# Relative bias table, overflow loop, last down weights and last norm of a decoder layer on one core

## Chip, core and metric

The kernel runs on one core of a Trainium2 chip. The metric is device time in microseconds (us). TensorE (PE) does the matmuls, PEld are its weight loads, VectorE is DVE, ScalarE is ACT, GpSimd is POOL; SyncE (SP) issues nearly all DMAs. Every engine works through its own instructions in order.

## What is computed

One layer of a decoder on 256 tokens of width 1024, in float32: attention with eight heads and a causal relative bias, a norm, then a mixture of 32 experts of which each token takes four, and a last norm. The reference, cut:

```python
s_own = einsum('bhqd,bhjd->bhqj', qc, ko) * scale + rel_t[:, t5_bucket(rel_own)]
s_own = where(rel_own >= 0, s_own, -inf)          # causal
x = layer_norm(alpha * x + softmax(s_own) @ v @ w_out)
top_logit, top_e = top_k(x @ w_router + b_router, 4); gate = softmax(top_logit)
# per expert: h = x @ w_gu[e] + b_gu[e]; act = swiglu(h); y = act @ w_down[e] + b_down[e]
out = layer_norm(alpha * x + sum(gate * y))
```

## The kernel before

The order of all work is written out by hand. Weights come in chunks of 2 MB, one for each slot: a pool has 13 slots of 128 x 4096 floats, of which two hold long-lived tiles (`BT_xT`, `QT_KTt`) through the expert part, so that up to 11 hold weights. `todo` is the list of chunks in order: six blocks of the input projection (`in`), two of the output projection, then for each expert four chunks `gu` (gate and up) and two `dn` (down). `prefetch` issues the next chunk on SP whenever a slot is free beyond `reserve[0]`; `done` frees a slot and calls it. Each DMA is given one of eight semaphores in turn (`DMAHW0` to `DMAHW7` in the order below) and is issued when the previous one on that semaphore has landed, so that at most eight are under way.

Attention: `split` turns each weight block into a high and a low part (a cast on ACT, a subtraction on DVE); steps n = 0 to 11 of a loop (`proj_qk`, `proj_v`) multiply half a block each. The bias reaches the softmax through DRAM: `rel_bias` multiplies the one-hot buckets by the table on PE, `rel_bias_out` writes the result as 8 rows of 383 numbers to `rd`, and `rel_bias_in` reads it back as the tile `BT`, 128 partitions of 8 heads x 256, each partition one place further on. Write and read are issued by ACT in steps n = 2 and 3. `softmax` of the first head needs `BT` in step 5.

Experts: each has 64 places. `stage1` multiplies by gate and up, `swiglu` makes the activation, `act_T` transposes it into `aT`, `stage2` multiplies by down into `Y`. Experts go in pairs; `pair_scatter` adds a pair's result to `acc` by a matmul with the gates `GT`, during the next pair. Choices beyond 64 places would be done by `more_blocks`, a loop whose number of turns is read from `n_i` at run time by every engine; with these inputs it has no turn. It stands behind expert 31, and is followed by the last pair's scatter and the last norm (`mean_neg`, `variance`, `centre`, `inverse_root`, `finish`), mostly on DVE. `spread_gain` makes the norm's gain and bias of all partitions during expert 30. The last chunk (`dn` of expert 31) is fetched in four pieces.

Of the kernel before, what the change touches and what calls it, by code (L numbers as in the profile page):

```python
# [11 lines left out]
F32 = mybir.dt.float32  # L12
# [11 lines left out]
NE, TOPK = 32, 4  # L24
# [36 lines left out]
def tile_decoder_layer(ctx: ExitStack, tc, a, out):  # L61
# [78 lines left out]
    def prefetch():  # L140
        while todo and W_SLOTS - used[0] > reserve[0]:
            fetch(1 if len(todo) > 1 else 4)
# [83 lines left out]
    BT, QT, KTt = (t.rearrange("p (h s) -> p h s", h=H) for t in (BT, QT, KTt))  # L226
# [3 lines left out]
    rrow = hp.tile([H, 383], F32, name="rrow")  # L230
# [6 lines left out]

    xT3 = xT.rearrange("p (k s) -> p k s", k=KT)
# [18 lines left out]
    nc.vector.memset(rrow[:, 0:127], NEG)  # L257
    nc.vector.memset(zeros, 0.0)
    rd = dr.tile([H, 383], F32, name="rd")

    def rel_bias():
        pr = bank("tp2")
        nc.tensor.matmul(pr[:H, :256], rb, oh, start=True, stop=True)
        nc.vector.tensor_copy(rrow[:, 127:383], pr[:H, :256])
        nc.sync.dma_start(c, a["consts"])
        nc.sync.dma_start(router.rearrange("p k e -> p (k e)"), a["router"])
# [87 lines left out]
    def softmax(hh):  # L354
# [39 lines left out]
    for n in range(12):  # L394
# [4 lines left out]
        if n == 1:  # L399
            rel_bias()  # L400
            reserve[0] = 1
            prefetch()
        if n == 2:
            rel_bias_out()
        if n == 3:
            rel_bias_in()
# [248 lines left out]
    def pair_gather(OH):  # L655
        xg = biases[:, :1024].rearrange("p (k c) -> p k c", k=KT)
# [34 lines left out]
    def act_T(act):  # L691
# [5 lines left out]
    def stage2(aT, chunk, swap, Y, after, apart=False):  # L697
        banks = [bank(n) for n in (("yp", "hg") if apart else ("yp",))]
        y_ps = [banks[s * apart][s * 64:(s + 1) * 64] for s in range(2)]
# [8 lines left out]
        for s, copy in enumerate((nc.scalar.copy, nc.vector.tensor_copy if apart else nc.scalar.copy)):  # L708
            copy(Y[s * 64:(s + 1) * 64, s ^ swap, :], y_ps[s])  # L709
# [77 lines left out]
    def more_blocks():  # L787
# [4 lines left out]
        GT2 = spare[:, 1024:1536].rearrange("p (b t c) -> p b t c", b=2, t=2)  # L792
        itn = small("itn", 1)
# [3 lines left out]
        with tc.For_i(0, n_reg, 1):  # L797
# [23 lines left out]
            OH = mp.tile([128, 2, 2, CAP], F32, name="OH")  # L821
            Gd = mp.tile([128, 2, 2, 2, CAP], F32, name="Gd")
# [6 lines left out]
            xg, quarter = pair_gather(OH)  # L829
# [21 lines left out]
            for t in range(2):  # L851
                for cb in range(2):
# [9 lines left out]
    for p in range(NE // 2):  # L862
        ahead_pair = p + 1 < NE // 2
        for s in range(2):
# [14 lines left out]
            reserve[0] = int(e == 14)  # L879
# [7 lines left out]
            if e == 21:  # L887
                overflow_list()
            if look_ahead:
# [12 lines left out]
            if e == NE - 2:  # L902
                gb2, sq = halves(slot("gb2_sq"))
                spread_gain()
            stage2(aT, lambda j: take(("dn", e, j)), s, Y, lambda j: done(("dn", e, j)), apart=e == NE - 1)
    more_blocks()
    nc.scalar.preload_act_table(AF.Sqrt)


    sm = [mp.tile([128, 8], F32, name=f"sm{t}") for t in range(2)]  # L910
    sq = sq[:, :D]

    def mean_neg(t):
        for cb in range(2):
            po = o_tile()
            nc.tensor.matmul(po, GT[:, cb, t, :], Y[:, cb, :], start=True, stop=True)  # L916
            d = acc[:, t, HALVES[cb]]
            nc.vector.scalar_tensor_tensor(d, po, 1.0, d, op0=OP.mult, op1=OP.add,  # L918
                                           accum_out=sm[t][:, cb:cb + 1])
        nc.vector.tensor_scalar(sm[t][:, 2:3], sm[t][:, 0:1], sm[t][:, 1:2], -1.0 / D, op0=OP.add, op1=OP.mult)  # L920

    def variance(t):
        nc.scalar.activation(sq, acc[:, t], AF.Square, bias=sm[t][:, 2:3], accum_out=sm[t][:, 3:4])
        nc.scalar.activation(sm[t][:, 4:5], sm[t][:, 3:4], AF.Sqrt, scale=1.0 / D, bias=eps)

    def centre(t, s, on_vector=False):
        d, m, g = acc[:, t, s], sm[t][:, 2:3], gb2[:, :D][:, s]
        if on_vector:
            nc.vector.scalar_tensor_tensor(d, d, m, g, op0=OP.add, op1=OP.mult)  # L929
        else:  # L930
            nc.scalar.activation(d, d, AF.Identity, bias=m)
# [71 lines left out]
```

## Time and profile before

| | us |
|---|---|
| median of 3 runs | 1087.15 (1087.0 to 1087.31) |
| profiled execution, its own time | 1087.11 |
| its span, first to last instruction | 1085.3 |
| PE busy | 975.1 (90%) |
| DVE busy | 265.6 (24%) |
| ACT busy | 180.5 (17%) |
| moved by DMA | 425.74 MB, mean 392 GB/s |

Rows are read so: an entry such as `PE o L310` is an engine, the tile it writes and the source line; what stands in brackets at the end of a row is the engine's idle time before it and what ended it. Starts count from the first instruction of the span. Lines are those of the kernel before.

### The profile page before, as it was taken

The page shows a single profiled execution, that of the slowest core. Times are in us where ns is not written, and L with a number is a line of the kernel's source. Part 1 is how long each engine was busy: PE and PEld are TensorE (multiplying, and loading weights), DVE is VectorE, ACT ScalarE, POOL GpSimd, SP SyncE. Part 2 cuts the span into 40 slices and gives each one's busy share as a digit, 9 for nine tenths or more (in the row PEclk, how much of TensorE's full clock was granted, in tenths as well). Part 3 has the DMA queues.
Part 4 walks back from the last instruction along what each step waited for, and adds up shares of the span by engine and source line. Part 5 has one row for each costly group of instructions (what it writes and reads, how often), then busy time and mean ns, then how long its engine had stood idle before and what let it go on. Part 6 is the DMA issues. An engine that isn't in the chain of part 4 may idle for free. (4 is left out here: it accounts for less than half of the span.)

```text
span 1085.3 us, 11473 instructions
## 1 busy us (share of the span) xinstructions
PE 975.1 (90%) x4886; PEld 450.4 (41%) x4886; DVE 265.6 (24%) x555; ACT 180.5 (17%) x345; POOL 15.7 (1%) x10
## 2 busy tenths in 40 slices
PE   9649989999999999888989889999989898988893
PEld 8648764334343443232424243343423243333331
DVE  5237562121222211112121232212111212121104
ACT  5126431101011110010101010011101010101112
POOL 0000030000000000000000000000000000000001
PEclk9869989999999999999999989999999999999997
DMA  9964579999999999999999999999999999999981
GB/s 358 422 243 152 161 297 406 428 427 428 428 426 428 428 425 430 427 427 429 426 429 428 413 423 426 428 428 427 427 428 427 428 429 428 428 428 426 429 372 40
DMA packets 33204, 425.74 MB, mean 392 GB/s; under 512 B 3672, under 2 KB 5120, under 8 KB 7456
## 3 DMA queue, kind: packets, MB, share of 16 engines
q1 hardware_dynamic: 31824, 422.87, 92.8%
q10 hardware_dynamic: 1328, 2.11, 0.6%
q8 instruction: 40, 0.66, 0.2%
q14 instruction: 12, 0.10, 0.0%
HBM read 423.91 MB, written 1.06 MB: 392 GB/s over the span
## 5 line engine op out<-in xcount | busy, mean ns | idle before, releaser
L677 PE MATMUL hg<-w,QT_KTt 128*64 128x512 f32 x960 | 250.8, 599 | 54.5 <-DMA w<-in_w_gu 54.2
L677 PE MATMUL hu<-w,QT_KTt 128*64 128x512 f32 x960 | 248.6, 594 | 0.0
L705 PE MATMUL yp<-w,QT_KTt 128*64 128x512 f32 x1008 | 226.8, 595 | 1.3 <-ACT QT_KTt L695 1.3
L684 DVE TENSOR_SCALAR QT_KTt<-hg 128x512 f32<-128x512 f32 x32 | 22.1, 692 | 665.5 <-PE hg L677 665.5
L677 PEld LDWEIGHTS hg<-w,QT_KTt 128*64 128x64 f32 x960 | 66.0, 137 | 194.9 <-issue 127.0
L705 PEld LDWEIGHTS yp<-w,QT_KTt 128*64 128x64 f32 x1008 | 70.6, 137 | 142.3 <-issue 127.9
L677 PEld LDWEIGHTS hu<-w,QT_KTt 128*64 128x64 f32 x960 | 71.2, 137 | 135.7 <-issue 135.7
L685 ACT ACTIVATE QT_KTt<-QT_KTt 128x512 f32<-128x512 f32 x32 | 20.1, 629 | 477.7 <-DVE QT_KTt L684 477.7
L709 ACT COPY QT_KTt<-yp 64x512 f32<-64x512 f32 x63 | 36.5, 580 | 233.4 <-PE yp L705 225.9
L663 PEld LDWEIGHTS tp<-OH,BT_xT 128*128 128x128 f32 x480 | 58.4, 199 | 12.0 <-issue 11.2
L663 PE MATMUL tp<-OH,BT_xT 128*128 128x128 f32 x480 | 62.7, 286 | 0.0
L165 DVE TENSOR_TENSOR whl<-w,whl 128x1024 fp32r<-128x1024 f32 (+1 forms) x36 | 41.2, 1187 | 29.4 <-ACT whl L176 29.4
L310 PE MATMUL o<-xhl,whl 128*128 128x256 f32 x48 | 15.0, 312 | 25.1 <-DVE QT_KTt L320 24.5
L176 ACT CAST whl<-w 128x1024 fp32r<-128x1024 f32 (+1 forms) x36 | 32.7, 954 | 11.3 <-DMA w<-in_w_in 4.7
L569 DVE TENSOR_SCALAR QT_KTt<-tp,c 128x128 f32<-128x128 f32 x60 | 20.5, 405 | 44.1 <-PE tp L663 44.1
L733 PE MATMUL tp<-QT_KTt 128*128 128x512 f32 x60 | 30.7, 593 | 0.0
L733 PE MATMUL o<-QT_KTt 128*128 128x512 f32 x60 | 29.8, 618 | 0.0
L571 ACT ACTIVATE QT_KTt<-tp,c 128x128 f32<-128x128 f32 x60 | 22.6, 457 | 36.3 <-PE tp L663 36.3
L695 ACT COPY QT_KTt<-tp 128x512 f32<-128x512 f32 x32 | 19.2, 600 | 42.9 <-PE tp L694 35.9
L686 DVE TENSOR_SCALAR hu<-hu 128x512 f32<-128x512 f32 x32 | 22.4, 700 | 3.1 <-PE hu L677 0.2
L694 PE MATMUL tp<-c,QT_KTt 128*128 128x128 f32 x128 | 20.0, 280 | 3.4 <-DVE QT_KTt L688 3.2
L688 DVE SCALAR_TENSOR_TENSOR QT_KTt<-hu,QT_KTt 128x512 f32<-128x512 f32 x32 | 22.1, 691 | 1.1
(258 smaller groups left out, 758.7 us busy)
## 6 DMA issues: line engine op xcount, KB each, us to landing
w<-in_w_gu SPq DMA_DIRECT2D x128, 2048.0 KB, 39.1
w<-in_w_dn SPq DMA_DIRECT2D x63, 2048.0 KB, 39.1
w<-in_w_in SPq DMA_DIRECT2D x3, 2048.0 KB, 21.1
w<-in_w_in SPq DMA_DIRECT2D x4, 1024.0 KB, 11.1
w<-in_w_out SPq DMA_DIRECT2D x2, 2048.0 KB, 28.3
w<-in_w_dn SPq DMA_DIRECT2D x4, 512.0 KB, 31.8
w<-in_w_in SPq DMA_DIRECT2D x4, 256.0 KB, 5.7
w<-in_w_in SPq DMA_DIRECT2D x2, 512.0 KB, 8.5
```

The lines of the kernel that those rows point to most:

```text
L165: nc.vector.tensor_tensor(lo[:, s], w[:, s], hi[:, s].bitcast(F32), op=OP.subtract)
L176: nc.scalar.copy(o, i)
L569: nc.vector.tensor_scalar(o, i, g, b, op0=OP.mult, op1=OP.add)
L571: nc.scalar.activation(o, i, AF.Identity, scale=g, bias=b)
L663: nc.tensor.matmul(ps[:, k * 128:(k + 1) * 128], h[:, t, kk * 128:(kk + 1) * 128], OH[:, t].rearrange("p s c -> p (s c)"), start=t == 0, s ...
L677: nc.tensor.matmul(hgu[i][s * 64:(s + 1) * 64], xg(k), w[:, kk, q * 512:(q + 1) * 512], start=False, stop=k == KT - 1)
L684: nc.vector.tensor_scalar(g7, hgu[0], LIMIT, None, op0=OP.min)
L686: nc.vector.tensor_scalar(u7, u7, LIMIT, -LIMIT, op0=OP.min, op1=OP.max)
L688: nc.vector.scalar_tensor_tensor(sg, u7, 1.0, g7, op0=OP.add, op1=OP.mult)
L705: nc.tensor.matmul(y_ps[s], aT[:, kk % 4, kk // 4, :], w[:, k, HALVES[s ^ swap]], start=kk == 0, stop=kk == KT - 1)
L709: copy(Y[s * 64:(s + 1) * 64, s ^ swap, :], y_ps[s])
L733: nc.tensor.matmul(po, GT[:, cb, t, :], Y[:, cb, :], start=True, stop=True)
```

## The change

Four parts, in the order of the program.

1. The bias table is kept with the head as inner index: `rd` has 383 rows of 8 numbers and `BT` is read as 128 runs of 256 x 8 numbers. The table and the one-hot rows are fetched by ACT at the very start, the two matmuls and the copy come ahead of the first casts, and two writes on ACT (127 rows that stand for the masked places, then 128 x 2 rows) are followed by the read on SP, between two halves of the prefetch. In the softmax the bias is read with a step of 8.
2. `more_blocks` is called behind expert 25; `reserve` is 3 from expert 24 on, for the three slots that the loop takes, and 0 afterwards. Its tiles `OH`, `Gd` and `xg` lie in its spare slot.
3. The order of weights at the end is `gu` 30, `gu` 31, `dn` 30, and then `dl`: expert 31's down weights stored as four blocks of 2 x 128 columns, two blocks to a chunk, each block a DMA of its own. `stage1` of expert 31 precedes `stage2` of expert 30; `stage2_columns` and `add_columns` then go through the blocks (0, 1), (2) and (3).
4. The norm's statistics are taken block by block (`Stats`, bn_stats), and the last steps are shared: the low halves on DVE (`scaled`), the high halves on ACT, POOL and DVE (`normal`, `shifted`), with stores on SP and ACT.

```diff
-    for e in range(NE):
+    for e in range(NE - 2):
         todo += [("gu", e, k) for k in range(GU)] + [("dn", e, j) for j in range(DN)]
+    todo += [("gu", e, k) for e in (NE - 2, NE - 1) for k in range(GU)]
+    todo += [(n, e, j) for n, e in (("dn", NE - 2), ("dl", NE - 1)) for j in range(DN)]
...
+    nc.scalar.dma_start(rb, a["rel_bias"])
+    nc.scalar.dma_start(oh, a["onehot"])
...
-    rd = dr.tile([H, 383], F32, name="rd")
-    def rel_bias():
-        pr = bank("tp2")
-        nc.tensor.matmul(pr[:H, :256], rb, oh, start=True, stop=True)
-        nc.vector.tensor_copy(rrow[:, 127:383], pr[:H, :256])
...
-    def rel_bias_out():
-        nc.scalar.dma_start(rd, rrow)
-    def rel_bias_in():
-        nc.scalar.dma_start(BT, bass.AP(tensor=rd.tensor, offset=rd.offset, ap=[[1, 128], [383, H], [1, S]]))
+    rd = dr.tile([383, H], F32, name="rd")
+    def rel_rows(row, ap):
+        return bass.AP(tensor=rd.tensor, offset=rd.offset + row * H, ap=ap)
+    pr = bank("yp")
+    for i in range(2):
+        nc.tensor.matmul(pr[:, i * H:(i + 1) * H], oh[:, i * 128:(i + 1) * 128], rb, start=True, stop=True)
+    nc.vector.tensor_copy(rrow[:, :2], pr[:, :2 * H].rearrange("p (i h) -> p i h", i=2))
+    nc.scalar.dma_start(rel_rows(0, [[H, 127], [1, H]]), rrow[:127, 2])
+    nc.scalar.dma_start(rel_rows(127, [[H, 128], [128 * H, 2], [1, H]]), rrow[:, :2])
+    fetch(2)
+    nc.sync.dma_start(BT_rows, rel_rows(0, [[H, 128], [1, S * H]]))
+    fetch(2)
...
-            reserve[0] = int(e == 14)
+            reserve[0] = {14: 1, 24: 3, 25: 3}.get(e, 0)
...
+            if e >= NE - 2:
+                break
...
+            stage2(aT, lambda j: take(("dn", e, j)), s, Y, lambda j: done(("dn", e, j)))
+            if e == 25:
+                reserve[0] = 0
+                more_blocks()
-    more_blocks()
+    act_T(act, aT_even)
+    pair_scatter(GT, Y, 1, False, (1,))
+    GT = pair_slots_T(Gd)
+    spread_gain()
+    e = NE - 1
+    hgu = stage1_bias(sel[:, e:e + 1].to_broadcast([3 * NE, CAP]))
+    stage1(lambda k: xg[:, k, CAP:], lambda k: take(("gu", e, k)), hgu, lambda k: done(("gu", e, k)))
+    act = swiglu(hgu)
...
+    stage2(aT_even, lambda j: take(("dn", e - 1, j)), 0, Y, after_even)
...
+    stage2_columns(aT, (0, 1), ("hg", "hu"))
+    add_columns((0, 1), ("o0", "o1"))
+    stage2_columns(aT, (2,), ("tp0", "tp1"))
+    add_columns((2,), ("tp2", "yp"))
+    stage2_columns(aT, (3,), ("hg", "hu"))
+    add_columns((3,), ("o0", "o1"))
...
+    for st in stats:
+        st.root()
+    for t in range(2):
+        stats[t].finish()
+        normal(t)
+    for t in range(2):
+        scaled(t)
+    for t in range(2):
+        shifted(t)
```

The two functions that do a block of columns, cut:

```python
    def stage2_columns(aT, blocks, names):
...
        for i, b in enumerate(blocks):
            w = take(("dl", NE - 1, b // 2))[:, b % 2].rearrange("p (k h c) -> p k h c", k=KT, h=2)
            for k in range(KT):
                for s in range(2):
                    nc.tensor.matmul(y_ps[s][:, i * 128:(i + 1) * 128], aT[:, k % 4, k // 4, :], w[:, k, s ^ 1],
                                     start=k == 0, stop=k == KT - 1)
        for s, copy in enumerate((nc.scalar.copy, nc.vector.tensor_copy)):
            copy(Y[s * 64:(s + 1) * 64, s ^ 1, cols], y_ps[s])
...
    def add_columns(blocks, names):
...
        for t in range(2):
            po = bank(names[t])[:, :2 * n].rearrange("p (b c) -> p b c", b=2)
            for cb in range(2):
                nc.tensor.matmul(po[:, cb], GT[:, cb, t, :], Y[:, cb, cols], start=True, stop=True)
            d = acc[:, t].rearrange("p (b c) -> p b c", b=2)[:, :, cols]
            nc.vector.tensor_tensor(d, po, d, op=OP.add)
            for cb in range(2):
                stats[t].add(stats[t].used, d[:, cb])
```

A block is thus 16 matmuls of 128 columns and its addition 4.

How the order moves, engine by engine. ACT at the start of the program, before; `xhl` and `whl` are the split input and weights, `DMAHW` with a number is a DMA's semaphore:

```order
L176 ACT_TABLE_LOAD
L176 CAST xhl<-BT_xT 128x256 [waits DMAHW0_49]
L176 CAST whl<-w 128x512 [waits DMAHW1_49]
L176 CAST xhl<-BT_xT 128x256 [waits DMAHW2_49]
L176 CAST whl<-w 128x512 [waits DMAHW3_49]
```

ACT at the same place now:

```order
L243 DMA rb<-in_rel_bias 32x8
L244 DMA oh_wg<-in_onehot 32x256
L271 DMA rd<-rrow 127x8 [waits DVE_49]
L272 DMA rd<-rrow 128x2x8 [waits DMAHW1_49,DVE_49]
L180 ACT_TABLE_LOAD
L180 CAST xhl<-BT_xT 128x256
L180 CAST whl<-w 128x512 [waits DMAHW3_49]
```

Four DMAs, the last of which waits for DVE's copy of the table, now stand ahead of the table load and the first cast.

SP early in the program now; the row of L274 is the read of `BT`, its waits are those for ACT's second write and for an earlier weight piece, and `DMAHW4` in the fourth row is the semaphore that ACT's first write of `rd` was given:

```order
L252 DMA w<-in_w_in 128x512 [waits DMAHW0_49]
L253 DMA BT_xT<-in_xT 128x1024 [waits DMAHW2_49]
L142 DMA w<-in_w_in 128x1024 [waits DMAHW3_49]
L142 DMA w<-in_w_in 128x1024 [waits DMAHW4_49]
L142 DMA w<-in_w_in 128x2048 [waits DMAHW5_49]
L142 DMA w<-in_w_in 128x2048 [waits DMAHW6_49]
L274 DMA BT_xT<-rd 128x2048 [waits DMAHW7_49,DMAHW1_49]
L142 DMA w<-in_w_in 128x2048 [waits DMAHW0_49]
```

The read of `BT` has come from ACT's queue to SP's, ahead of the third weight block.

SP where the loop stands, before (at the end of all fetches; `n_i` is the number of turns):

```order
L138 DMA w<-in_w_dn 128x1024 [waits DMAHW4_49,PE_49]
L138 DMA w<-in_w_dn 128x1024 [waits DMAHW5_49]
L138 DMA w<-in_w_dn 128x1024 [waits DMAHW6_49]
L138 DMA w<-in_w_dn 128x1024 [waits DMAHW7_49]
L795 TENSOR_LOAD n_i [waits DVE_49]
L797 COMPARE_AND_BRANCH
L797 UNCONDITIONAL_BRANCH [waits SP_sequencer_49,DMAHW0_49,DMAHW1_49,DMAHW2_49,DMAHW3_49,DMAHW4_49,DMAHW5_49]
```

SP where it stands now, with the loop's own transfers left out:

```order
L142 DMA w<-in_w_dn 128x4096 [waits DMAHW7_49,PE_49]
L142 DMA w<-in_w_gu 128x4096 [waits DMAHW0_49,PE_49]
L142 DMA w<-in_w_gu 128x4096 [waits DMAHW1_49,PE_49]
L811 TENSOR_LOAD n_i [waits DVE_49]
L813 COMPARE_AND_BRANCH
L813 UNCONDITIONAL_BRANCH [waits SP_sequencer_49,DMAHW2_49,DMAHW3_49,DMAHW4_49,DMAHW5_49,DMAHW6_49,DMAHW7_49]
...
L142 DMA w<-in_w_gu 128x4096 x2
L142 DMA w<-in_w_dn 128x4096
L142 DMA w<-in_w_dn 128x4096 [waits PE_49]
L142 DMA w<-in_w_gu 128x4096 [waits PE_49] x4
L142 DMA w<-in_w_dn 128x4096 [waits DMAHW0_49,PE_49]
```

The loop now stands in the stream of weights: the two `gu` rows ahead of it are the first half of expert 27, and the rows behind it begin with the second half.

## Rows read from the trace of the kernel before

**Rows 1.** The page's second part: GB/s moved in 40 slices of the span.

```profile
GB/s 358 422 243 152 161 297 406 428 427 428 428 426 428 428 425 430 427 427 429 426 429 428 413 423 426 428 428 427 427 428 427 428 429 428 428 428 426 429 372 40
```

**Rows 2.** Waits over the span: who waited for whom, us in total, times, longest.

```profile
DVE p L359 <- DMA BT_xT<-rd: 28.5, 1, 28.5
...
PE hg L677 <- DMA w<-in_w_gu: 54.2, 48, 2.3
```

**Rows 3.** Timeline of PE: start, us, operation, [idle before <- releaser].

```profile
68.86 0.55 PE L310 MATMUL o<-xhl,whl 128*128 128x256 f32 x1 [24.49 <-DVE QT_KTt L320]
```

**Rows 4.** Windows: length, busy us (count) of each engine, PEclk, DMA share, GB/s.

```profile
44.40:68.80 24.40, 0.00 (x0) 0.00 (x0) 1.56 (x6) 0.71 (x3) 0.00 (x0) 0.57 0.85 353
...
68.80:71.60 2.80, 2.74 (x13) 2.77 (x14) 1.98 (x5) 2.69 (x6) 0.00 (x0) 0.50 0.01 3
...
170.00:400.00 230.00, 227.56 (x1120) 89.48 (x1118) 44.03 (x88) 29.01 (x56) 0.00 (x0) 1.00 1.01 428
...
860.00:1050.00 190.00, 169.75 (x830) 67.36 (x828) 30.68 (x62) 22.25 (x43) 0.00 (x0) 1.00 1.01 427
```

**Rows 5.** The page's DMA issues: count, KB of each, us from issue to landing.

```profile
w<-in_w_gu SPq DMA_DIRECT2D x128, 2048.0 KB, 39.1
...
BT_xT<-rd ACTq DMA_DIRECT2D x1, 1024.0 KB, 37.1
...
rb<-in_rel_bias SPq DMA_DIRECT2D x1, 1.0 KB, 7.5
```

**Rows 6.** Timeline of ACT in the first 31 us, and PE's warm-up matmuls.

```profile
0.74 1.28 ACT L176 ACT_TABLE_LOAD   x1 [0.74 <-PEq L995]
...
1.06 4.21 PE L256 MATMUL tp<-ones 128*128 128x128 f32 x18 [1.06 <-DVE ones L252]
...
3.32 0.40 ACT L176 CAST xhl<-BT_xT 128x256 fp32r<-128x256 f32 x1 [1.30 <-DMA BT_xT<-in_xT]
...
24.78 0.55 ACTq L269 DMA_DIRECT2D rd<-rrow  x1
...
30.00 0.39 ACTq L272 DMA_DIRECT2D BT_xT<-rd  x1
```

**Rows 7.** Timeline of DVE: where stage 1 of experts 0, 9, 31 ends.

```profile
172.04 0.69 DVE L684 TENSOR_SCALAR QT_KTt<-hg 128x512 f32<-128x512 f32 x1 [7.70 <-PE hg L677]
...
401.13 0.69 DVE L684 TENSOR_SCALAR QT_KTt<-hg 128x512 f32<-128x512 f32 x1 [19.39 <-PE hg L677]
...
1051.59 0.69 DVE L684 TENSOR_SCALAR QT_KTt<-hg 128x512 f32<-128x512 f32 x1 [23.74 <-PE hg L677]
```

**Rows 8.** The DMA queue's own waits between 1030 and 1090 us (SP).

```profile
SPq L797 <- SPq L797: 21.0, 6, 4.9
```

**Rows 9.** Line 797, the loop: count, ns min/median/max, first and last start.

```profile
L797 PEldq COMPARE_BRANCH  x3: 97/196/3549, 1059.2 to 1067.7; - x3
```

**Rows 10.** Timeline of SP: issues of expert 27's four gate and up transfers.

```profile
877.13 15.00 SPq L138 DMA_DIRECT2D w<-in_w_gu  x4
```

**Rows 11.** Timeline of PE: the first matmul of expert 26 and of 31.

```profile
887.36 0.39 PE L577 MATMUL hg<-bgu,sel 96*64 96x512 bf16 x2
...
1037.70 0.39 PE L577 MATMUL hg<-bgu,sel 96*64 96x512 bf16 x2
```

**Rows 12.** Timeline of PE: spread of gains, stage 2, the last matmuls.

```profile
1026.97 3.89 PE L740 MATMUL tp<-c 128*128 128x128 f32 x32
...
1030.79 7.09 PE L705 MATMUL yp<-w,QT_KTt 128*64 128x512 f32 x32
...
1067.94 5.70 PE L916 MATMUL o<-QT_KTt 128*128 128x512 f32 x8 [5.00 <-issue]
```

**Rows 13.** Timeline of DVE: statistics of the first norm; the last scalings.

```profile
148.93 1.34 DVE L190 BATCH_NORM_STATS2 st_a<-BT_xT 128x6 f32<-128x512 f32 x3
...
1076.90 2.42 DVE L945 SCALAR_TENSOR_TENSOR BT_xT<-BT_xT,sm,gb_sq 128x512 f32<-128x512 f32 x2
...
1080.85 1.41 DVE L945 SCALAR_TENSOR_TENSOR BT_xT<-BT_xT,sm,gb_sq 128x512 f32<-128x512 f32 x2
```

More of the change, by code (lines that the diff above doesn't have):

```diff
@@ L141, in prefetch @@
         while todo and W_SLOTS - used[0] > reserve[0]:
-            fetch(1 if len(todo) > 1 else 4)
+            fetch(2 if todo[-1][0] == "dl" else 1)
     def take(key):
@@ L229, in tile_decoder_layer @@
     oh, wg = oh_wg[:32], oh_wg.rearrange("p (k e) -> p k e", k=KT)
-    rrow = hp.tile([H, 383], F32, name="rrow")
+    rrow = hp.tile([128, 3, H], F32, name="rrow")
     zeros = hp.tile([128, 128], BF, name="zeros")
@@ L653, in pair_gates, with pair_gather @@
         return Gd
[L655 to L656 removed]
+    def pair_gather(OH, xg=None):
+        xg = (biases[:, :1024] if xg is None else xg).rearrange("p (k c) -> p k c", k=KT)
         def quarter(q):
@@ L695, in act_T, with stage2 @@
         nc.scalar.copy(aT, ps.rearrange("p (j s c) -> p j s c", j=4, s=2))
-    def stage2(aT, chunk, swap, Y, after, apart=False):
-        banks = [bank(n) for n in (("yp", "hg") if apart else ("yp",))]
-        y_ps = [banks[s * apart][s * 64:(s + 1) * 64] for s in range(2)]
+    def stage2(aT, chunk, swap, Y, after):
+        ps = bank("yp")
+        y_ps = [ps[s * 64:(s + 1) * 64] for s in range(2)]
         for j in range(DN):
@@ L707, in stage2 @@
             after(j)
-        for s, copy in enumerate((nc.scalar.copy, nc.vector.tensor_copy if apart else nc.scalar.copy)):
-            copy(Y[s * 64:(s + 1) * 64, s ^ swap, :], y_ps[s])
+        for s in range(2):
+            nc.scalar.copy(Y[s * 64:(s + 1) * 64, s ^ swap, :], y_ps[s])
+    def stage2_columns(aT, blocks, names):
+        n = len(blocks) * 128
+        cols = slice(blocks[0] * 128, blocks[0] * 128 + n)
+        y_ps = [bank(names[s])[s * 64:(s + 1) * 64, :n] for s in range(2)]
+        for i, b in enumerate(blocks):
+            w = take(("dl", NE - 1, b // 2))[:, b % 2].rearrange("p (k h c) -> p k h c", k=KT, h=2)
+            for k in range(KT):
+                for s in range(2):
+                    nc.tensor.matmul(y_ps[s][:, i * 128:(i + 1) * 128], aT[:, k % 4, k // 4, :], w[:, k, s ^ 1],
+                                     start=k == 0, stop=k == KT - 1)
+        for s, copy in enumerate((nc.scalar.copy, nc.vector.tensor_copy)):
+            copy(Y[s * 64:(s + 1) * 64, s ^ 1, cols], y_ps[s])
     def pair_slots_T(Gd, GT=None):
@@ L828, in more_blocks @@
                                                 op0=OP.is_equal, op1=OP.mult)
-            xg, quarter = pair_gather(OH)
+            xg, quarter = pair_gather(OH, spare[:, 2304:3328])
             quarter(0)
@@ L901, in tile_decoder_layer @@
                 Gd = pair_gates(e + 1, OH)
[L902 to L905, printed above, removed]
-    more_blocks()
-    nc.scalar.preload_act_table(AF.Sqrt)
[L910 to L931, printed above, removed]
-            nc.gpsimd.tensor_tensor(d, d, g, op=OP.mult)
@@ L966 @@
+    for t in range(2):
[3 more added lines that the diff above has]
+        scaled(t)
+    for t in range(2):
+        shifted(t)
 def kernel(**inputs):
```

87 lines of the change are left out of this document (44 added, 43 removed).

## Prediction, made before the run

> **What bounds the kernel now.** I read the page's slices first, then the waits, then the stretches that they point to. The slices show three parts: transfers run at full rate for two slices, fall to 152 GB/s in slices 3 to 6, and hold some 428 from slice 8 to the end [rows 1]. So the transfers bound nearly everything after 170 us, and what can be won lies where they pause and behind the last of them. The waits name the cause of the pause: DVE stood 28.5 us for the bias tile, once [rows 2]. PE behind it was idle for 24.49 us and started again at 68.86 [rows 3], at half its clock (0.50) for another 2.8 us [rows 4].
>
> In the expert part two paces are to be seen. From 170 to 400 us PE is busy 227.56 of 230 us: it works off the chunks that had been fetched ahead, and nine experts take 401.13 - 172.04 = 229.1 us [rows 7], 25.46 each, while the transfers already run at 428 [rows 4]. Later it is busy 169.75 of 190 us [rows 4] and waits for `w_gu` (54.2 us in all) [rows 2]: the transfers' pace. Their step is read from SP, which may have eight under way and issues one when one lands: four issues in 15.00 us, so (15.00 - 0.3) / 3 = 4.9 us [rows 10], six chunks 29.4 us an expert. One lands 39.1 us after its issue, eight steps [rows 5].
>
> **The start.** Why the bias came so late: its write was issued at 24.78, its read at 30.00 [rows 6], and the read, 1 MB in 1024 pieces on ACT's queue, took 37.1 us to land [rows 5], the length of eight whole chunks. It now goes as 128 long pieces on SP's queue, behind two weight blocks, at about 14 us; even if it took 37.1 us from there it would land at 51, and taking its turn among the weights it lands near 25. Its consumer, softmax 0, is due when PE has done step 4, about 38. So the hole of 24.5 goes, and with it half of the 2.8 us at half clock, 1.2 (13 matmuls at twice their time). What is late next in the hole's place is the evacuation of the banks that step 6 writes again, some 0.5 us of copies. The transfers, one hole poorer at 44 us, catch up in the stretch of slices 3 to 6, which had some 56 us to spare (the slices' shortfall against 428): the slots were full there, and will be again before the experts. So the expert part begins earlier by the whole amount.
>
> Against it stands ACT's first cast. It was at 3.32 [rows 6]; now it waits for the table (one piece like the 7.5 us of `rb` at the worst [rows 5], 3 to 4 us ahead of all traffic), then for PE's warm-up, which ends at 5.3 [rows 6], the small matmuls and DVE's copy (0.7), a DMA issue (0.4 as at 30.00) and ACT's own table load of 1.28 [rows 6]: 7.6. Of these 4.3 us most is made up, since ACT and DVE used to wait for the pieces of the first block; counting their casts and subtractions on from 7.6 leaves PE's second step 1.1 us late. Bounds: 0 and 4.3. Sum of the start: -24.5 - 1.2 + 0.5 + 1.1 = -24.1 us. The strided read in the softmax is not in the trace; between nothing and double time for 16 short operations it stays hidden, as DVE has room beside PE there.
>
> The write of 127 rows has a row of its own in the order: SP's piece of the first block waits for its landing. By the nearest rows (`rb`, 32 rows, 7.5 us [rows 5]) it lands by 9, and the piece is needed at 13. The Trainium skill ("DMA: Bandwidth & Descriptors", section "Why a DMA increments its semaphore by 16 and not by 1") says that a transfer is spread over the largest number of engines up to 16 that divides its rows, so that 127 partitions go through one; no run here shows it yet. By that the sum would be about 1.5 us worse, and, at its worst, the second rival below.
>
> **The loop.** Before, SP reached line 797 at 1035 and waited there for six transfers to land, 21.0 us, the longest 4.9, although the loop has no turn [rows 8]; then the engines met, and PE was held 5.0 us [rows 12], 3.5 of it in one branch [rows 9]. This lay at the end, where all had to land anyway. Now SP meets the same waits with the queue full. What is ahead of it: with `reserve` at 3 there are eight chunks, to the second of expert 27. That one was issued at 877.13 + 4.9 = 882.0 [rows 10] and lands 39.1 later [rows 5], at 921.1; the transfers are busy without a break until then, so this holds in the new order too (all times here are those of before, to be moved by the -24.1). PE is at expert 26's first matmul at 887.36 [rows 11] and can do nothing else, all its work being behind the branch. DVE, ACT and POOL wait in the same place, and SP's next issues are queued behind it. The branch's 3.5 us lie under the wait; what is left of the 5.0 is 1.4. PE restarts at 922.5, 35.1 later, and loses 1.2 to the clock as after the hole: +36.3.
>
> The Trainium skill ("Runtime: NRT & Kernel Launch", section "Instruction fetch mechanics") says that a taken branch to code not at hand costs a fetch by DMA. The 3.5 us of [rows 9] agree; were a second one met behind the wait, the sum would be 3.5 us higher.
>
> Part of it comes back. At 922.5 eight chunks lie in their slots, and the transfers restart a few us later with 28 chunks left, 28 x 4.9 = 137 us: they end at about 1062, before PE needs the last block. So PE goes at its own pace to the end. From expert 26's first matmul to expert 31's were 1037.70 - 887.36 = 150.3 us [rows 11]; at its own pace they are 5 x 25.46 and the spread of gains, 3.9 [rows 12], 131.2: -19.1. Loop and pace together: +17.2.
>
> **The end.** From expert 31's first matmul to the end of the span were 1085.3 - 1037.7 = 47.6 us. Now that matmul comes before stage 2 of expert 30 (7.1 [rows 12]) and behind four transposes more (0.7): 6.4 earlier. After it: stage 1, 1051.59 - 1037.70 [rows 7, 11] and 0.6 for its other half, 14.3; stage 2 of expert 30 and the transposes, 7.7, which cover the swiglu. Then the columns: 64 pairs of matmul passes; such passes of 128 columns come every 3.89 / 32 = 0.122 us [rows 12], so 7.8 for pairs that run together and 15.6 if they do not; the same columns in one piece took 7.1. Together is nearer, since the halves of stage 2 already run in pairs: 9.0. Copies between, 3 x 0.4, and the additions' matmuls, 3.9: 14.1. Behind the last matmul DVE has an addition, two statistics (a 512-wide one and two 256-wide took 1.34 [rows 13], so 0.2 each for 128), two aggregates and twice five tiny operations, 3.6 in all; four scalings between 0.7 and 1.2 (2.42 for two beside POOL [rows 13]), 4.0; two additions, 1.4; and store and close, 3.0 as from DVE's last row (1080.85 + 1.41) to 1085.3 [rows 13]. That is 12.0, and 14.3 + 7.7 + 14.1 + 12.0 - 6.4 = 41.7 against 47.6: -5.9. What falls away is the 5.0 of the loop; the block order itself gains nothing, as it is PE that is late, not the last chunk.
>
> **Sum**, against the profiled execution's own 1087.1 (the median is 1087.15): -24.1 + 36.3 - 19.1 - 5.9 = -12.8, **1074.3 us**.
>
> **Rivals.** *The loop drains nothing* (its zero turns skip the waits). For it: PE's rows at 797 are short but for one. Against: SP's 21.0 us with no turn made. Then the transfers bound to the end: the last lands at about 1058 (1035 + 21 and two quarter chunks of 1.2), and behind it come one block (2.2 + 0.4 + 1.0) and the 12.0, so 1073.7 instead of 1085.3, and 1087.1 - 24.1 - 11.6 = 1051.4. *The small write takes the place of the long read*: its 127 rows go one by one through one engine, each after a weight packet, as the old read's pieces did (1024 over 16 engines, 64 on each, 37.1 / 64 = 0.58 us a piece), and SP's queue and step 1 stand behind it. At half that time, since the early packets are smaller, it lands at 1.7 + 127 x 0.29 = 39 and the piece behind it at 42 instead of 13: with what step 1 had in hand 27 us more, 1101, slower than before. It decides from 0.2 us a row on; below that, as I expect (small packets, and the queue runs empty while SP waits), it costs 1 to 3 us and stays in my forecast.
>
> **How the numbers follow.** Forecast 0.85, no drain 0.10, late write 0.05. The forecast's own range: upper ends are 3 for the start, 3.5 for a second branch, 6.6 for the columns and 1 for the scalings, not all at once; lower ends 1.6, 1.9 and 1: 1062 to 1085, which holds all but 0.05 of its 0.85. That makes 0.8, and the two rivals stay outside. A measurement can tell 0.2%, 2 us, from no change: faster 0.92, same 0.03, slower 0.05.
>
> **What would show it.** PE busy without a break at 40 to 70 us, first matmul near 9 instead of 5.4; the bias tile landing before 38. SP waiting at line 813 for six to eight landings, some 35 us, with PE idle from about 863 to 898 and transfers pausing for a few us after it. From there no wait of PE for `w_gu`, and experts 25.5 apart. The last transfer landing some 10 us before PE's last block. It would be wrong if PE passes line 813 within 6 us, or if it waits for weights again behind it.

## The result, and the profile after

The changed kernel takes 1076.98 us (median), the kernel before 1087.31 in the same runs: a ratio of 0.990 (95% interval 0.989 to 0.992), faster by about 1%. Forecast were 1074.3 us with a range of 1062 to 1085. The profiled execution took 1077.43 us, its span 1075.7.

The page's slices of the changed kernel come first: PE's busy tenths, the granted clock, and GB/s.

```profile
PE   8999899999999998989888799999998815999994
...
PEclk8999899999999999999999999899999966999998
...
GB/s 361 426 324 224 268 365 428 427 428 427 428 428 428 428 427 427 428 428 426 427 428 428 411 427 429 426 428 426 428 427 428 428 424 327 429 428 427 428 261 40
```

Against [rows 1] the sag behind the second slice is shallower and the full rate is reached earlier. A new dip stands in slice 34 (327), and in the slice ahead of it PE's digit falls to 1: PE is idle there while the transfers still run (424). The waits say what it is (who waited for whom, us in total, times, longest; PE's first, then those of SP's DMA queue):

```profile
PE hg L677 <- DMA w<-in_w_gu: 40.0, 35, 2.3
...
PE hg L577 <- issue: 34.9, 1, 34.9
```

```profile
SPq L813 <- SPq L813: 28.3, 6, 4.9
...
SPq L813 <- DMA w<-in_w_gu: 9.6, 1, 9.6
```

The 28.5 us that DVE stood for the bias tile in [rows 2] are gone. In their place is one wait of PE, 34.9 us, while SP stands at line 813, the loop, for one landing after another. Stretches of the changed kernel as windows (length, busy us of PE, PEld, DVE, ACT and POOL with counts, PEclk, DMA share, GB/s):

```profile
8.00:12.00 4.00, 3.58 (x15) 3.35 (x16) 3.91 (x8) 4.00 (x8) 0.00 (x0) 0.50 1.02 349
...
40.00:70.00 30.00, 30.00 (x215) 28.21 (x214) 19.64 (x41) 15.95 (x36) 0.00 (x0) 1.00 1.01 427
864.90:899.60 34.70, 0.00 (x0) 0.00 (x0) 0.00 (x0) 1.12 (x2) 0.00 (x0) 0.54 0.85 363
899.70:905.50 5.80, 5.80 (x16) 1.77 (x18) 0.00 (x0) 0.00 (x0) 0.00 (x0) 0.50 0.95 345
905.50:1040.00 134.50, 134.50 (x670) 54.63 (x668) 25.83 (x50) 17.41 (x33) 0.00 (x0) 1.00 1.00 422
```

Read against [rows 4]: the hole at 44 to 69 us is filled (PE busy 30.00 of 30). From 864.9 to 899.6 PE does nothing at a DMA share of 0.85. Behind it PE is busy 134.50 of 134.50 us, where it was busy 169.75 of 190 before: its own pace, as forecast. Not forecast is the 0.50 in the first row. The timelines of PE and DVE give the points from which the terms of the sum can be read (start, us, operation; for DVE's line 684 the page of that line, with the first and the last start):

```profile
8.43 0.58 PE L313 MATMUL o<-xhl,whl 128*128 128x256 f32 x1 [2.98 <-ACT whl L180]
...
40.21 0.39 PE L353 MATMUL hg<-QT_KTt 128*128 128x128 f32 x2
...
899.67 0.64 PE L577 MATMUL hg<-bgu,sel 96*64 96x512 bf16 x2 [34.86 <-issue]
...
1027.09 0.41 PE L577 MATMUL hg<-bgu,sel 96*64 96x512 bf16 x2
```

```profile
L684 DVE TENSOR_SCALAR QT_KTt<-hg x32: 691/692/693, 149.1 to 1040.6; 128x512 f32<-128x512 f32 x32
```

Expert 0's stage 1 ends at 149.1 instead of 172.04 [rows 7]; expert 26 begins at 899.67 instead of 887.36, expert 31 at 1027.09 instead of 1037.70 [rows 11]; the span ends at 1075.7 instead of 1085.3. Between these four points the spans differ like this:

| stretch | forecast | measured |
|---|---|---|
| to the end of expert 0's stage 1 | -24.1 | 149.1 - 172.0 = -22.9 |
| to expert 26's first matmul (the loop's wait) | +35.1 | 12.3 + 22.9 = +35.2 |
| to expert 31's first matmul (pace -19.1, clock +1.2, order -6.4) | -24.3 | 127.4 - 150.3 = -22.9 |
| to the end of the span (48.1 against 47.6) | +0.5 | 48.6 - 47.6 = +1.0 |
| sum | -12.8 | -9.6 |

### The profile page after: what moved, and what is told of

Its sections match the earlier page's. It is cut to its first block, busy times and chain, and to the rows that moved or that the text cites. A ratio compares the mean times of both kernels' runs of the same rounds, so it can differ in the third digit from the quotient of the medians.

```text
span 1075.7 us, 11703 instructions
## 1 busy us (share of the span) xinstructions
PE 971.2 (90%) x5000; PEld 455.9 (42%) x5000; DVE 271.9 (25%) x569; ACT 178.3 (17%) x343; POOL 16.1 (1%) x10
## 4 chain that ended last, share of the span: by engine, by line
DMA 55%; PE 39%; DVE 4%; ACT 1%; issue 1%; SPq 0%; DVEq 0%; ACTq 0%
DMA w<-in_w_gu 40%; DMA w<-in_w_dn 14%; PE hg L677 8%; PE hu L677 8%; PE yp L705 8%; PE tp L663 2%; PE o L747 1%; DVE whl L169 1%; PE tp L747 1%; DMA QT_KTt<-in_b_gu 1%; PE tp L315 1%; PE tp L314 1%; PE tp L313 1%; PE o L313 1%; PE o L315 1%; ACT whl L180 1%
## 5 line engine op out<-in xcount | busy, mean ns | idle before, releaser
L705 PE MATMUL yp<-w,QT_KTt 128*64 128x512 f32 x960 | 212.6, 595 | 0.7 <-ACT QT_KTt L695 0.7
L705 PEld LDWEIGHTS yp<-w,QT_KTt 128*64 128x64 f32 x960 | 66.3, 137 | 133.3 <-issue 119.9
L577 PE MATMUL hg<-bgu,sel 96*64 96x512 bf16 x64 | 12.7, 390 | 34.9 <-issue 34.9
L577 PEld LDWEIGHTS <-sel 96*64 96x64 bf16 x128 | 7.3, 112 | 53.2 <-issue 53.1
## 6 DMA issues: line engine op xcount, KB each, us to landing
w<-in_w_dl SPq DMA_DIRECT2D x4, 1024.0 KB, 29.5
```

Of the source, the lines that this page charges most:

```text
L705: nc.tensor.matmul(y_ps[s], aT[:, kk % 4, kk // 4, :], w[:, k, HALVES[s ^ swap]], start=kk == 0, stop=kk == KT - 1)
```

## The experiments

**Theory.** The new bias path is worth some 23 us, whole, because transfers bind behind it. The loop, though it makes no turn, waits for all transfers under way, and PE, whose work is all behind the loop, waits with it. What that costs depends on how many are under way, and on how many experts are left in which PE can catch up. **Rival:** the loop is cheap; what is missing went in the start or in the new end. The kernel before ran at 1088.8 to 1089.0 us in these runs, so the ratios are the safer numbers.

| kernel | us | ratio to before | 95% interval |
|---|---|---|---|
| changed kernel | 1076.98 | 0.990 | 0.989 to 0.992 |
| bias_only | 1064.28 | 0.978 | 0.976 to 0.979 |
| loop_only | 1101.2 | 1.011 | 1.010 to 1.013 |
| no_loop | 1057.97 | 0.972 | 0.970 to 0.973 |
| loop_end | 1067.54 | 0.980 | 0.979 to 0.982 |
| early_loop | 1061.83 | 0.975 | 0.973 to 0.977 |
| short_queue | 1062.63 | 0.976 | 0.974 to 0.977 |
| warm_longer | 1074.66 | 0.987 | 0.985 to 0.989 |
| rd_on_sp | 1072.48 | 0.986 | 0.984 to 0.987 |
| gain_early | 1057.18 | 0.971 | 0.970 to 0.973 |
| best | 1059.55 | 0.973 | 0.972 to 0.974 |

### One part at a time: the bias, the loop

The kernel before with the new bias path alone (its core; order, reserve, loop and end as before):

```diff
-    def rel_bias_in():
-        nc.scalar.dma_start(BT, bass.AP(tensor=rd.tensor, offset=rd.offset, ap=[[1, 128], [383, H], [1, S]]))
...
+    nc.scalar.dma_start(rel_rows(0, [[H, 127], [1, H]]), rrow[:127, 2])
+    nc.scalar.dma_start(rel_rows(127, [[H, 128], [128 * H, 2], [1, H]]), rrow[:, :2])
+    fetch(2)
+    nc.sync.dma_start(BT_rows, rel_rows(0, [[H, 128], [1, S * H]]))
```

> The kernel before with the bias edit alone: early one-hot product, the table with the head as inner index, the read in 128 long pieces, the strided read in the softmax. Theory A (the start's gain is whole, and the moved loop takes it back): the slots are full before the experts and transfers bind from there on, so the 23.0 us that the first expert came earlier in the changed kernel (149.1 against 172.0 at the end of its stage 1) reach the end: 1087.3 - 23.0 = 1064.3, bounds 1062 to 1066. Theory B (the start's gain is lost on its own way, because transfers that bind later do not come earlier by as much as PE does): somewhere between 1075 and 1087.

Measured: 1064.28 us, as theory A has it. The agreement to the digit is luck: the kernel before took 1088.83 in these runs, so the gain is 24.5 and not 23.0. The gain of the start is worth all that it was taken for, and the rest of the change takes half of it back.

The kernel before with the loop alone moved (an excerpt, without the loop's tiles in its spare slot):

```diff
-            reserve[0] = int(e == 14)
+            reserve[0] = {14: 1, 24: 3, 25: 3}.get(e, 0)
...
+            if e == 25:
+                reserve[0] = 0
+                more_blocks()
-    more_blocks()
```

> The kernel before with the overflow loop alone moved behind expert 25, with the reserve of three slots there, and the old bias and the old end. Theory A (the loop waits for every transfer under way, and PE with it): 34.9 us of wait and 2.8 of half clock as in the changed kernel, less 19.1 for PE's own pace behind it, less the 5.0 that the loop took at the end: 1087.3 + 37.7 - 19.1 - 5.0 = 1100.9, bounds 1097 to 1104. Theory B (the loop is cheap where it stands, and what is missing in the changed kernel went in the start or the new end): 1087.3 - 5.0 = 1082, or up to 1087.

Measured: 1101.2 us, slower than before by 1.1%, 0.3 us from theory A. Against the kernel before of the same runs (1088.83) that is +12.4, where theory A had +13.6. The waits of PE and of SP's queue show the same idle time without any of the other parts:

```profile
PE hg L577 <- issue: 34.8, 1, 34.8
```

```profile
SPq L799 <- SPq L799: 28.3, 6, 4.9
...
SPq L799 <- DMA w<-in_w_gu: 9.6, 1, 9.6
```

The rival falls here: moving the loop is the part that costs.

### The loop's price: without it, at the end, early, with a shorter queue

The changed kernel without the loop:

```diff
-            reserve[0] = {14: 1, 24: 3, 25: 3}.get(e, 0)
+            reserve[0] = int(e == 14)
...
-            if e == 25:
-                reserve[0] = 0
-                more_blocks()
```

> The changed kernel without the overflow loop (it leaves out the handling of experts with more than 64 tokens, which makes no turn with these inputs) and without its three slots. Theory A: transfers bind to the end, 1087.3 - 23.0 - 11.6 = 1052.7, bounds 1049 to 1056, with PE waiting for weights again in the last experts and the last transfer landing near 1035 in the trace. Theory B (the wait at the loop is made up almost whole by PE's faster pace behind it): 1070 or above.

Measured: 1057.97 us. Theory A's direction, but 2 us beyond its bounds. The loop where the change put it costs 19.0 us of time (1076.98 - 1057.97; by the ratios 0.0186 of 1088, 20). The miss of 5 us is in the end. Windows of this kernel (columns as above):

```profile
1000.00:1028.50 28.50, 28.50 (x150) 12.67 (x150) 5.95 (x10) 6.01 (x9) 0.00 (x0) 1.00 0.99 418
...
1034.00:1042.00 8.00, 6.96 (x84) 5.78 (x83) 5.58 (x16) 0.52 (x2) 0.00 (x0) 1.00 0.00 0
```

I had let the end follow the last transfer by one block. The last transfer is in by 1034, as I had worked out (no GB/s from there on), but PE is busy without a break from 1000 to 1028.5 and works until 1042: without the loop the end is PE's, not the transfers'. How little separates the two, gain_early shows below.

The changed kernel with the loop behind the weights (an excerpt, without the place for expert 31's activations):

```diff
-            reserve[0] = {14: 1, 24: 3, 25: 3}.get(e, 0)
+            reserve[0] = int(e == 14)
...
-            if e == 25:
-                reserve[0] = 0
-                more_blocks()
...
     stage2(aT_even, lambda j: take(("dn", e - 1, j)), 0, Y, after_even)
+    more_blocks()
```

> The changed kernel with the loop back behind the weights: between stage 2 of expert 30 and the column blocks of expert 31, when no transfer is left to be issued (expert 31's transposed activations get a place of their own, since the loop's body would write over them). Theory A: the price of the loop is the transfers under way that PE does not need yet, and here it needs all of them: last landing near 1035, 5.0 for the branch and the meeting of the engines, then 26.8 us from the first block to the end of the span as in the changed kernel (1048.9 to 1075.7) and 1.7 outside it: 1068.5, bounds 1064 to 1072. Theory B (the loop costs some 35 us wherever it stands): 1077 or above.

Measured: 1067.54 us (theory A 1068.5). PE's timeline shows the loop where all transfers are needed anyway, and a window shows PE behind it:

```profile
1036.33 0.48 PE L720 MATMUL hg<-w,tail 128*64 128x128 f32 x1 [6.40 <-DMA w<-in_w_dl]
```

```profile
1036.00:1040.00 4.00, 3.67 (x34) 3.67 (x36) 0.00 (x0) 1.28 (x1) 0.00 (x0) 0.50 0.02 4
```

6.40 us of idle time instead of 34.86: the same loop, with nothing under way that PE did not need. It is not the whole price here. Behind the 6.40 us PE works at 0.50, and from the first block to the end of the span (1065.8) pass 29.5 us and not 26.8: the wait and the clock, 6.4 + 2.7, are nearly all of the 9.6 us by which this kernel is behind no_loop. It is also 3.3 us behind bias_only, which has the old order of weights, the loop behind expert 31 and the old norm: with this loop in front of it, the new end gains nothing.

The changed kernel with the loop behind expert 11:

```diff
-            reserve[0] = {14: 1, 24: 3, 25: 3}.get(e, 0)
+            reserve[0] = {10: 3, 11: 3, 14: 1}.get(e, 0)
...
-            if e == 21:
+            if e == 9:
                 overflow_list()
...
-            if e == 25:
+            if e == 11:
```

> The changed kernel with its loop (and the list it needs, at expert 9) moved from behind expert 25 to behind expert 11, with the same three reserved slots. Theory A: what PE loses at the loop it makes up at about 3.9 us an expert while transfers bind, so 20 experts behind it are more than enough for 37.7, where six gave back 19.1; what stays is the pause of the transfers themselves, some 5 us (one of 8 transfers after another falls out, then 2.7 us with none). Without the loop the time was 1058.0; so 1063, bounds 1060 to 1066, with PE waiting for weights again in the last experts. Theory B (the 35 us are lost wherever the loop stands ahead of the end): 1077 or above.

Measured: 1061.83 us. PE's timeline, then its waits, then GB/s in 40 slices:

```profile
483.34 0.64 PE L577 MATMUL hg<-bgu,sel 96*64 96x512 bf16 x2 [34.53 <-DMA w<-in_w_gu]
```

```profile
PE hg L677 <- DMA w<-in_w_gu: 28.7, 27, 1.3
```

```profile
GB/s 345 426 356 222 254 364 429 425 430 427 426 429 427 428 427 427 428 428 349 431 425 428 413 426 429 427 426 429 427 426 429 427 425 429 429 425 429 428 423 78
```

PE stands as long as before, 34.53 us, and yet the time is 15 us better than with the loop at 25. It catches up and then waits for weights again (27 waits). What remains is the transfers' own pause: slice 19 has 349 instead of 428, and 79 / 428 of a slice of 26.5 us is 4.9 us. Against no_loop the time is 3.9 us longer.

The changed kernel with a shorter queue at the loop:

```diff
-            reserve[0] = {14: 1, 24: 3, 25: 3}.get(e, 0)
+            reserve[0] = {14: 1, 24: 7, 25: 7}.get(e, 0)
```

> The changed kernel with seven slots kept back at experts 24 and 25 instead of three, so that four transfers are under way at the loop and not eight. Theory A (PE waits 4.9 us for each transfer under way): the idle time of PE at the loop falls from 34.9 to 34.9 - 4 x 4.9 = 15.3 us; the transfers run on without a gap until then, so PE's own pace no longer sets the end but the transfers' pause does: 1058.0 + 5 = 1063, bounds 1060 to 1067. Theory B (the loop's own price, not the number of transfers under way, makes the 34.9): idle time about 35 again, time 1077.

Measured: 1062.63 us. PE's waits:

```profile
PE hg L677 <- DMA w<-in_w_gu: 44.9, 40, 2.1
...
PE hg L577 <- DMA w<-in_w_gu: 15.0, 1, 15.0
```

Four transfers fewer under way, 34.9 - 15.0 = 19.9 us less idle time: 5.0 for each, against 4.9 forecast. With early_loop this settles the mechanism: each transfer that has still to land when PE reaches the loop costs PE one step of the transfers (34.9 / 4.9 is about seven of them, 15.0 / 4.9 about three), and it costs time as far as PE has no experts left in which to make it up.

### The start: clock, and ACT's queue

Why were the first scores 3.1 us late (40.21, in the trace of before 37.15) and not 1.1? Their row of before:

```profile
37.15 0.39 PE L350 MATMUL hg<-QT_KTt 128*128 128x128 f32 x2
```

The changed kernel with more dummy matmuls:

```diff
+    for i in range(13):
+        nc.tensor.matmul(warm[:, :128], ones, ones, start=i == 0, stop=i == 12)
     nc.vector.tensor_copy(rrow[:, :2], pr[:, :2 * H].rearrange("p (i h) -> p i h", i=2))
```

> The changed kernel with 13 more dummy matmuls behind the two small ones of the bias table, which fill PE's idle 2.98 us before its first projection. Theory A (the start slipped by 3.1 us and not by 1.1 because the granted clock fell to 0.50 from 7.8 to 14.6 us after that idle time): granted clock 1.00 from 8 to 15 us, expert 0's stage 1 ends at 147.1 instead of 149.1, time 1075. Theory B (the casts of ACT and DVE, not PE, set the pace of the first step): 149.1 and 1077 whatever the clock.

Measured: 1074.66 us. A window, the first scores, and the ends of stage 1 (the line is 686 here):

```profile
8.00:12.00 4.00, 3.78 (x31) 3.52 (x31) 3.50 (x7) 4.00 (x8) 0.00 (x0) 1.00 0.99 350
```

```profile
38.33 0.39 PE L355 MATMUL hg<-QT_KTt 128*128 128x128 f32 x2
```

```profile
L686 DVE TENSOR_SCALAR QT_KTt<-hg x32: 690/692/693, 147.2 to 1038.6; 128x512 f32<-128x512 f32 x32
```

The clock is 1.00 where it was 0.50, and expert 0 is ready at 147.2 instead of 149.1, 1.9 us earlier (2.0 forecast). What is left of the slip is 38.33 - 37.15 = 1.2, the 1.1 that the prediction had for the casts. So the casts were sized rightly, and a term for the clock was missing. The Trainium skill ("TensorE: Matmul & The Clock Gate", section "Part 1: The HAM clock gate (the "warmup" mystery)") says that the low level is the engine's default and that activity releases it; the two rows agree.

How much the clock costs is less sure than this pair makes it look. Six other kernels here have the start of the changed kernel, with 2.95 to 2.98 us of idle time of PE at the same place, and in their profiled executions expert 0 is ready between 147.6 (no_loop) and 149.4 (short_queue):

```profile
L684 DVE TENSOR_SCALAR QT_KTt<-hg x32: 691/692/693, 147.6 to 1020.3; 128x512 f32<-128x512 f32 x32
```

```profile
L684 DVE TENSOR_SCALAR QT_KTt<-hg x32: 690/692/693, 149.4 to 1026.5; 128x512 f32<-128x512 f32 x32
```

So the dummy matmuls won between 0.4 and 2.2 us at expert 0; the medians of the runs differ by 2.3 (1076.98 and 1074.66). Nor does a 1.00 this early always mean full speed. The same window of early_loop:

```profile
8.00:12.00 4.00, 2.82 (x12) 2.60 (x13) 3.27 (x7) 3.99 (x9) 0.00 (x0) 1.00 1.00 364
```

PE does 12 matmuls in 2.82 us of work there, as slow as the 15 in 3.58 us at 0.50, while warm_longer does 31 in 3.78. The number of matmuls has to be read together with the clock.

The changed kernel with the two writes issued by SP:

```diff
-    nc.scalar.dma_start(rel_rows(0, [[H, 127], [1, H]]), rrow[:127, 2])
-    nc.scalar.dma_start(rel_rows(127, [[H, 128], [128 * H, 2], [1, H]]), rrow[:, :2])
+    nc.sync.dma_start(rel_rows(0, [[H, 127], [1, H]]), rrow[:127, 2])
+    nc.sync.dma_start(rel_rows(127, [[H, 128], [128 * H, 2], [1, H]]), rrow[:, :2])
```

> The changed kernel with the two writes of the bias table issued by SP behind its first pieces instead of by ACT, so that ACT's table load and first casts don't queue behind the one that waits for PE and DVE. Theory A (ACT's late first cast, 7.45 instead of 3.32, is the cause of the whole slip): first cast near 3.5, first matmul near 5.5, expert 0's stage 1 ends near 146.1 instead of 149.1, time 1074. Theory B (the pieces of the first block set the pace, or the writes on SP hold up the weights): 149 or later, 1077 or above.

Measured: 1072.48 us. The first cast of ACT, the first scores, and the ends of stage 1:

```profile
3.46 0.40 ACT L180 CAST xhl<-BT_xT 128x256 fp32r<-128x256 f32 x1 [0.51 <-DMA BT_xT<-in_xT]
```

```profile
36.09 0.39 PE L353 MATMUL hg<-QT_KTt 128*128 128x128 f32 x2
```

```profile
L684 DVE TENSOR_SCALAR QT_KTt<-hg x32: 690/692/693, 144.2 to 1035.2; 128x512 f32<-128x512 f32 x32
```

The whole slip goes, and a little more: expert 0 is ready 4.9 us earlier than in the changed kernel, where 3.0 were forecast. Of the 4.9, 4.1 are there at the first scores (36.09 instead of 40.21), which thus come 1.1 us ahead of those of the kernel before. Why the surplus is there stays open; the last kernel below, with the same start, shows less of it (146.3).

### The end without the loop, and all together

The kernel without the loop, with the spread of gains where PE waits (an excerpt, without the lines of no_loop and the slot kept back for the gains at experts 26 and 27):

```diff
+            if e == NE - 4:
+                tail = slot("tail")
+                gb2 = tail[:, :2 * D]
+                spread_gain()
             stage2(aT, lambda j: take(("dn", e, j)), s, Y, lambda j: done(("dn", e, j)))
...
     GT = pair_slots_T(Gd)
-    spread_gain()
```

> The changed kernel without the overflow loop (it leaves out the handling of experts with more than 64 tokens, which makes no turn with these inputs), and with the spread of the last norm's gains (32 matmuls, 3.6 us) moved from between experts 30 and 31 to expert 28, where PE waits for weights. Theory A (without the loop the end is bound by PE, which is busy without a break from 995 us on, behind the last pieces of the gate and up weights, and not by the last transfer at about 1033): 1058.0 - 3.6 = 1054.4, bounds 1053 to 1056. Theory B (the last transfers set the end): 1058, no change.

Measured: 1057.18 us, 0.8 better, not 3.6; the runs of the two kernels overlap, so it can be nothing. The number is nearer to theory B, but DVE's line 684 and PE's waits from 960 us on point to other transfers than the last.

```profile
L684 DVE TENSOR_SCALAR QT_KTt<-hg x32: 690/691/692, 148.1 to 1017.8; 128x512 f32<-128x512 f32 x32
```

```profile
PE hg L677 <- DMA w<-in_w_gu: 3.4, 4, 1.3
PE yp L705 <- DMA w<-in_w_dn: 1.9, 2, 1.3
```

Stage 1 of expert 31 ends 2.5 us earlier (1017.8; without the edit 1020.3). Then PE, which had no wait at all from 1000 on, waits 1.9 us for expert 30's down weights. Behind their landing it still has the second half of stage 2 and all the column blocks to do, more than the last two transfers take, 2 x 4.9. So the down weights of expert 30, and PE's work behind them, set the time: of the 3.6, 2.5 reach the end of stage 1, and 1.9 of these are lost in the new wait. That is read from the waits; no run of its own tested it.

The loop behind expert 11, the writes on SP and the early spread together (the three diffs above):

> The changed kernel with three edits together: the loop behind expert 11, the writes of the bias table on SP, the spread of gains at expert 28. If their gains are independent, since each lies in a stretch of its own and transfers or PE behind it carry the shift on: 1061.8 - 4.5 (the time of the kernel with the writes on SP, 1072.5, against 1077.0) - 3.6 = 1053.7, bounds 1052 to 1056. If the end of the early-loop kernel is bound by the last transfer, the 3.6 fall away: 1057.

Measured: 1059.55 us, 2.7% faster than before (2.6 to 2.8) and 17 us faster than the changed kernel, but 6 us short of the sum. The rows of DVE's line 684 and of PE's waits:

```profile
L684 DVE TENSOR_SCALAR QT_KTt<-hg x32: 690/692/693, 146.3 to 1020.3; 128x512 f32<-128x512 f32 x32
```

```profile
PE yp L705 <- DMA w<-in_w_dn: 1.9, 2, 1.3
```

Expert 0 is ready at 146.3, 2.4 us before that of early_loop (148.7), not 4.5; and the early spread runs into the same wait of 1.9 us as above. That the same start gave 144.2 in rd_on_sp is in part the clock. The window at 8 to 12 us of rd_on_sp, then that of this kernel:

```profile
8.00:12.00 4.00, 4.00 (x35) 4.00 (x35) 3.44 (x6) 3.22 (x6) 0.00 (x0) 1.00 0.90 322
```

```profile
8.00:12.00 4.00, 4.00 (x23) 4.00 (x22) 3.46 (x6) 3.34 (x6) 0.00 (x0) 0.57 0.85 331
```

PE is busy throughout in both, but at 0.57 it gets 23 matmuls done instead of 35, and the first scores come at 37.22 instead of 36.09: 1.1 of the 2.1 us. The other 1.0 lies behind the scores and stays open. From its first matmul up to this half clock PE had no idle time longer than 0.22 us, so a gap like that of the changed kernel is not the only thing that such a stretch can follow. What else sets it, no run here shows.

## Why the prediction was right, and where its terms were off

The forecast lay 2.7 us under the measured median, inside its range, and the mechanism of the bias path and of the loop held in the runs that tested it. The four stretches were off by 1.2, 0.1, 1.4 and 0.5 us, all the same way, so no error of one hid that of another; within the end, -0.7 and +1.5 did in part.

- **The start.** Right that the hole goes whole, that the transfers catch up, and that the slip of the casts is about 1.1 (1.2 in warm_longer). PE was unbroken at 40 to 70 us, its first matmul came at 8.43, and the bias was read, from 13.89 on (about 14 forecast), in 6.4 us where it took 37.1 [rows 5]:

```profile
BT_xT<-rd SPq DMA_DIRECT2D x1, 1024.0 KB, 6.4
```

  The term that was missing is the clock. I had moved the first matmul from 5.4 to near 9 and priced the casts, and not asked what the clock does while PE stands there: 2.98 us idle, then 0.50. By warm_longer it cost 1.9 in this execution; by the other executions of this start, 0.4 to 2.2.
- **The write of 127 rows.** SP's queue waited 0.5 us for it at line 142, and the sum had nothing for it:

```profile
SPq L142 <- DMA rd<-rrow: 0.5, 1, 0.5
```

  The rule of the Trainium skill ("DMA: Bandwidth & Descriptors", section "Why a DMA increments its semaphore by 16 and not by 1"), 127 rows through one engine, may hold, since the profile doesn't show how many engines took it; the 1.5 us that the prediction set against it, the 1 to 3 of its second rival (which no term of the sum holds), and that rival's late write are not there.
- **The loop.** 35.1 forecast, 35.2 measured: PE stood until the last of the transfers under way had landed, 4.9 us apart. Reading SP's 21.0 us at a loop without a turn [rows 8] as a wait for all landings was the step that carried the forecast. A second slow branch behind the wait, for which the 3.5 us of [rows 9] were set beside the sum, did not show: with 35.2 there is no room for it. What the Trainium skill ("Runtime: NRT & Kernel Launch", section "Instruction fetch mechanics") says of a taken branch, that it fetches code not at hand by DMA, is thus not seen behind the wait.
- **The clock behind the loop.** Sized 1.2 as after the hole, in whose place 2.8 us passed at 0.50 [rows 4]. Here PE worked the 5.8 us from 899.7 to 905.5 at 0.50, which cost 2.9: the passes of `hg` and `hu` came 0.43 us apart there and 0.21 behind it. This term is 1.7 too small.
- **The pace behind it.** Right: 134.50 of 134.50 us busy, no wait for `w_gu` any more, and the transfers end about 10 us ahead of the first column block, some 20 ahead of the last (the prediction's sign named the last for the 10):

```profile
1038.00:1040.00 2.00, 2.00 (x14) 0.56 (x10) 0.00 (x0) 0.00 (x0) 0.00 (x0) 1.00 0.31 127
1040.00:1048.80 8.80, 8.80 (x44) 3.01 (x42) 2.67 (x4) 2.50 (x3) 0.00 (x0) 1.00 0.01 2
1048.80:1062.20 13.40, 11.82 (x154) 10.24 (x150) 5.93 (x16) 2.04 (x5) 0.00 (x0) 1.00 0.01 1
1062.20:1075.70 13.50, 0.00 (x0) 0.00 (x0) 9.62 (x26) 2.22 (x4) 3.48 (x2) 0.64 0.21 78
```

- **The end.** Right in sum, 48.1 against 48.6. The column blocks with their additions take 13.4 (14.1 forecast), what follows them 13.5 (12.0). That the block order gains nothing is right too, since PE is late there.
- **Slips in the working**, none of which decided anything: half of 2.8 us is 1.4, not 1.2 (the 1.2 fits 13 matmuls that come 0.21 us apart there and 0.12 behind it, less than twice the time); 1051.59 - 1037.70 and 0.6 make 14.5, not 14.3; and the lower ends 1.6, 1.9 and 1 lead from 1074.3 to 1069.8, so that nothing is shown for the 1062 of the range.
- **The strided read** in the softmax was to lie between nothing and double. Its line takes longer, and stays hidden as forecast; DVE's rows of before and of after (ns min/median/max, first to last start):

```profile
L359 DVE SCALAR_TENSOR_TENSOR p<-hg,BT_xT x8: 282/353/418, 67.2 to 102.1; 128x128 f32<-128x128 f32 x4, 128x256 f32<-128x256 f32 x4
```

```profile
L362 DVE SCALAR_TENSOR_TENSOR p<-hg,BT_xT x8: 383/508/631, 43.8 to 79.9; 128x128 f32<-128x128 f32 x4, 128x256 f32<-128x256 f32 x4
```

- **The first rival**, no drain, had its price wrong: 1051.4, while the kernel without a loop takes 1058.0. Its step "behind the last transfer come one block and the 12.0" fails, because the new order puts stage 2 of expert 30 and all the blocks behind the last gate and up weights: PE was still at work on them until 1042, 8 us behind the last transfer.

## What to carry over

A loop on a register is not free where it makes no turn: here SP waited at it for every transfer under way, and all engines' work behind it waited too. The waits can be seen before anything is run: in the order above they stand on SP's branch. Put it where PE has many experts left to catch up while transfers bind, or keep the queue short ahead of it. And where an edit moves an engine's first work by some microseconds, ask what its clock does in the gap, as for any other wait.

## What the hardware did that I had not expected

- Behind an idle time of 2.98 us of PE, between dummy matmuls and its first real work, the granted clock stood at 0.50; with the gap filled it was 1.00 there, and expert 0 was ready 1.9 us earlier. In best a stretch at half clock (0.57 in the mean of 8 to 12 us) came without such a gap, and executions of one and the same start differ by up to 1.8 us at expert 0 (147.6 to 149.4).
- In the first 12 us a granted clock of 1.00 stood beside matmuls as slow as those at 0.50 (early_loop: 12 in 2.82 us of work; the changed kernel at 0.50: 15 in 3.58).
- The half clock behind the loop's 34.86 us of idle time lasted for 5.8 us of PE's work, behind the 24.49 us of [rows 3] for 2.8. Behind only 6.40 us, in loop_end, it cost some 2.7.
- The same megabyte was read in 6.4 us as 128 long pieces on SP's queue and in 37.1 as 1024 pieces on ACT's. Both the pieces and the queue differ, and no run separated them.
